# Narrow TensorE products of a hybrid decoder step widened to the whole array, and 32-column products of the recurrent stage issued together

## The chip, the cores and the metric

The kernel runs on one core of a Trainium2 chip. The metric is the device time of one execution in microseconds (us), the median over runs. TensorE is called PE in the profile, its load of the stationary operand PEld; DVE is VectorE, ACT ScalarE, POOL GpSimd, SP SyncE. In the names of products, out<-a,b has the stationary and the moving operand in either order; "128*32" are the rows and columns of the array that the stationary operand takes, and "x2" is a count of instructions. An fp32 product leaves two MATMUL records, an fp16 product one.

## The reference, cut to what matters

One layer of a decoder trunk for a prompt of 2048 tokens and a sample group of 8 sequences with 4 new tokens each (2080 token columns in all), with a past of 2048 tokens. RMSNorm, one combined input projection, two branches and an output projection:

```python
def layer_prompt(...):
    qA, kvA, gA, zA, qB, fB, iB, zB, mA, mB = project_inputs(x, norm_g, w_in)
    ctx = nsa_context(kc, vc, ks, vs, pos_k, w1_k, w2_k, pos_v, w1_v, w2_v)   # compressed blocks
    oA = nsa_attend(...) * silu(zA)       # compressed, top-8 selected and window branch, 8 heads, 2 K/V groups
    oB, S = hgrn2_branch(qB, fB, iB, zB, S0, lb, norm_g)                      # recurrence, 4 heads
    y = sigmoid(mA) * (oA @ w_ba) + sigmoid(mB) * (oB @ w_bb)
    return x + y @ w_out

# compress: out = silu(blk @ w1 + pos) @ w2, w2 is 64 x 64
# hgrn2_scan, in each chunk, with G the running sum of log decay:
A = einsum('bhtd,bhtsd,bhsd->bhts', qc, exp(D), kc)     # D = G_t - G_s for s <= t
o = einsum('bhtd,bhde->bhte', qc * exp(G), S) + einsum('bhts,bhse->bhte', A, vc)
S = exp(Gl)[..., None] * S + einsum('bhsd,bhse->bhde', kc * exp(Gl - G), vc)
```

## The kernel before

The matmuls run in fp16 pairs: an operand is split into a high and a low part (wh and wl, xh and xl), and a product is the sum of three. `mm` records a matmul, `pe.transpose` an fp32 transpose through the identity.

Stages, with their times in the profiled execution: the load of x (0 to 92 us), the compression of the sample's cache (92 to 382), bias rows (382 to 398), sample attention (398 to 640), the recurrent stage `hgrn` (640 to 1385), the start of the prompt's attention (1385 to 1600) and the rest of it with the output projection (1600 to 2467). The input projection has no stage of its own. Its products are fillers: `along(steps, ns)` goes through a stage's steps and after each issues so many nanoseconds of projection products. `feature` (L367) and `piece` (L427) make feature rows, `token` (L446) token rows.

The program is built in a context that schedules by a simulated timeline: each instruction gets a place on its engine by the code's order and by when its inputs are simulated to be ready, so code written together may be issued apart, with fillers between. Instructions under `tc.high_priority()` go ahead of others.

- `pow2_scale` (L188) turns 128 maxima, one per partition, into one power of two on all partitions: a transpose to a row (L190), DVE's maximum (L192), clamp and mask (L193, L195), a product of a one-row operand with ones (L196), DVE's scale and reciprocal (L198, L200). `pow2_of` (L216, L224) does the like for the columns of `mxs`.
- `token` multiplies 17 blocks of token rows; the last has 32.
- `hgrn` goes through 32 units (8 chunks of 256 tokens, 4 heads). `factors` makes five decay levels X0 to X4 on DVE, ACT and POOL (L717 to L721); `scores` makes, in each half of 128 tokens, one product of 64 columns and two of 32 (L740) and sixteen of 32 columns (L744) into the tile p4, from which ACT and DVE put together AT; `values` uses it. `sample_heads` does the same for the sample's 32 tokens.
- `compression` ends each of its 18 pieces with a product by w2 (L967 for keys, L977 for values), 64 rows of the array.
- `sample_attention`: `turn` transposes fetched keys (L1167), `piece` makes four products of 32 columns each, one per sequence, with 512 keys (L1190); `new` does the four new tokens (L1184).
- In the prompt phase `neg_row` (L1420) turns row maxima into rows of the queries' operand, through products with 2 or 4 stationary columns; `prep` makes the compressed branch: `cs` (L1551, L1552) scores nv = 8t + 8 compressed keys of query block t, `cpv` weighs the values, `sel` transposes the chosen blocks (L1577).

Of the kernel before, what the change touches and what calls it, by code (L numbers as in the profile page):

```python
# [10 lines left out]
F32 = mybir.dt.float32  # L11
# [42 lines left out]
def shape_constants():  # L54
# [48 lines left out]
    c["shift"] = np.tile((np.arange(256)[None, :] + np.arange(16)[:, None] == 127) * QS, (2, 1)).astype(np.float16)  # L103
# [27 lines left out]
def trunk_kernel(ctx: ExitStack, tc: tile.TileContext, A, O):  # L131
# [50 lines left out]
    ones1 = con.tile([1, 128], F32, name="ones1")  # L182
    ve.memset(ones1, 1.0)

# [3 lines left out]
    def pow2_scale(mx, pool, ps, tag):  # L188

        pe.transpose(ps[:1, 0:128], mx, ident)  # L190
        m1 = pool.tile([1, 1], F32, name=tag + "m", bufs=2)
        ve.tensor_reduce(m1, ps[:1, 0:128], axis=AX.X, op=OP.max)  # L192
        ve.tensor_scalar(m1, m1, TINY, None, op0=OP.max)  # L193
        mi = m1.bitcast(I32)
        ve.tensor_scalar(mi, mi, 0x7F800000, None, op0=OP.bitwise_and)  # L195
        mm(ps[:, 128:129], ones1, m1, True, True)  # L196
# [17 lines left out]
    def pow2_of(c0, n, ps, name):  # L214

        pe.transpose(ps[:n, 0:128], mxs[:, c0:c0 + n], ident)  # L216
# [39 lines left out]
    def make_projections(s2, st, sb):  # L256
# [3 lines left out]
        def quarter(hl, i):  # L260
            return xp.tile([128, 4352 if i == 3 else 4096], F16, name=f"x{hl}{i}")

        X4 = {hl: [quarter(hl, i).rearrange("p (k t) -> p k t", k=8) for i in range(4)] for hl in "hl"}
# [172 lines left out]
        def token(c0, n, names, ahead):  # L436
# [4 lines left out]
            for i, (t0, r) in enumerate(rows_of):  # L441
                ps = fps.tile([128, 512], F32, name="ps")[:r, :n]
                k = 0
                for kc in range(8):
                    for l, w in (("h", wh), ("h", wl), ("l", wh)):
                        mm(ps, xs(l, t0, r)[:, kc], w[:, kc], k == 0, k == 23)  # L446
                        k += 1
                    if kc == 3:
                        yield 1350
                if i == 1:  # L450
                    fetch(ahead)
# [157 lines left out]
    def hgrn():  # L609
        with ExitStack() as st:  # L610
# [32 lines left out]
            def gate_out(o_sb, zt, y, nt, r, h, t0):  # L643
# [3 lines left out]
                for j in range(nt):  # L647
                    pe.transpose(pt[:, j * 128:j * 128 + r], o_sb[:r, j], ident[:r, :r])
# [9 lines left out]

            def common(h, t0, n, L):
# [3 lines left out]
                def new(name, bufs=2):  # L663
                    return hp.tile([128, n], F32, name=name + sfx, bufs=bufs if n == NC or name == "E" else 1)
# [60 lines left out]
            def scores(u):  # L725
# [4 lines left out]
                ac.activation(u["kd"], pk[:, :NJ], AF.Copy)  # L730
                u["AT"] = []
                for j in range(NJ):
                    tj = slice(j * 128, (j + 1) * 128)
                    p4 = pa.tile([128, 4, 128], F32, name="p4")

                    near = p4[:, 1].rearrange("p (l t) -> p l t", l=4)
                    for li, L in enumerate(LEVELS[:2]):
                        X = u["Xs"][li][:, tj]
                        for s0 in range(0, 128, 2 * L):
                            mm(p4[s0:s0 + L, 0, s0 + L:s0 + 2 * L], X[:, s0:s0 + L], X[:, s0 + L:s0 + 2 * L], li == 0 or s0 == 64, True)  # L740
                    for li, (l, r) in enumerate([(x, x) for x in u["Xs"][2:]] + [(u["Bk"], u["Bq"])]):
                        for b in range(4):
                            bs = slice(j * 128 + 32 * b, j * 128 + 32 * b + 32)
                            mm(near[32 * b:32 * b + 32, li], l[:, bs], r[:, bs], li == 0 and b == 3, True)  # L744
                    AT = ATs.pop(0)
                    ATs.append(AT)
                    ac.activation(AT[:64, 2:], p4[:64, 0, 64:].rearrange("p (b t) -> p b t", t=32), AF.Copy)
                    for s0 in (0, 64):
                        ac.activation(AT[s0:s0 + 32, s0 // 32 + 1], p4[s0:s0 + 32, 0, s0 + 32:s0 + 64], AF.Copy)
# [37 lines left out]
            def sample_heads():  # L787
                for h in range(4):
                    G, qt, kt, Bq, Bk, Xo, Kd, eG = common(h, 2048, 32, 4)
                    v = hp.tile([32, 128], F32, name="vs_")  # L790
# [4 lines left out]
                    mm(pb[:32, :32], Bk, Bq, True, True)  # L795
                    AT = hp.tile([32, 32], F32, name="ATs")
# [3 lines left out]
                    mm(ov, v, AT, True, False)  # L800
                    for b in range(8):
                        mm(ov[:, 4 * b:4 * b + 4], S0[:, b], Xo[:, 4 * b:4 * b + 4], False, True)
                    oT = hp.tile([128, 32], F32, name="oT")
# [3 lines left out]
                    pe.transpose(pt[:32, :128], oT, ident)  # L807
                    o_sb = hp.tile([32, 1, 128], F32, name="o_s")
# [6 lines left out]
                    gate_out(o_sb, load_z(h, 2048, 32), y, 1, 32, h, 2048)  # L815
                    pk = po.tile([128, 512], F32, name="pk").rearrange("p (a b) -> p a b", a=4)
                    pe.transpose(pk[:32, 0], Kd, ident)
                    kd = hp.tile([32, 128], F32, name="kd_s")
# [3 lines left out]
                    for b2 in range(2):  # L822
                        vm = hp.tile([32, 4, 128], F32, name="vm", bufs=1)
# [3 lines left out]
                        mm(pu, kd, vm, True, True)  # L827
# [65 lines left out]
    def compression(seqs):  # L893
        with ExitStack() as st:
# [4 lines left out]
            for kind in "kv":  # L899
# [8 lines left out]
                w2 = cw.tile([64, 64], F32, name="w2" + kind)  # L908
                sy.dma_start(w2, A["cmp_w2_" + kind][0])
# [9 lines left out]
                ve.tensor_scalar(w2, w2, 0.5, None, op0=OP.mult)  # L919
                for s in seqs:  # L920
# [35 lines left out]
                    hb = cp.tile([64, 2, 128], F32, name="hb")  # L956
                    ac.activation(hb[:, :, :127], ph[64:128, :, 1:128], AF.Copy)
                    ve.memset(hb[:, :, 127:128], 0.0)
# [6 lines left out]
                    if kind == "k":  # L965
                        p2 = cps.tile([64, 2, 128], F32, name="p2")
                        mm(p2, w2, hb, True, True)  # L967
# [6 lines left out]
                    else:  # L974
                        p2 = cps.tile([128, 2, 64], F32, name="p2")
                        for g in range(2):
                            mm(p2[:, g], hb[:, g], w2, g == 0, True)  # L977
# [40 lines left out]
    def sample_attention():  # L1018

        with ExitStack() as st:  # L1020
# [154 lines left out]
            def logits(gb, X):  # L1175
# [5 lines left out]
                def new(kn):  # L1181
                    pq = sps.tile([128, 512], F32, name="ps", bufs=2)
                    for i, b in enumerate(bs):
                        mm(pq[32 * i:32 * i + 32, :4], queries(b), kn[:, 4 * b:4 * b + 4], True, True)  # L1184
                    return pq

                def piece(c, kts):
                    pq = sps.tile([128, 512], F32, name="ps", bufs=2)
                    for i, b in enumerate(bs):
                        mm(pq[32 * i:32 * i + 32], queries(b), kts[i], True, True)  # L1190
# [7 lines left out]
                for c in range(5):  # L1198
                    x = ready.pop(0)
                    kts = []  # L1200
                    for i in range(4):
                        kts.append(turn(x, i))
                        if i % 2:
                            yield
                            if i == 1 and last is not None:
                                piece(c - 1, last)
                    fetch()
                    last = kts
                    if c == 3:
                        pq = new(ksn)  # L1210
                        ve.scalar_tensor_tensor(S[:, 2048:], pq[:, :4], X["bm"][:, 32:33], bias[:, 128:132], op0=OP.add, op1=OP.add)
                        pq = new(kwn)
                        ve.tensor_add(Sw[:, 512:], pq[:, :4], bias[:, NB_S + 512:NB_S + NK_W])
# [189 lines left out]
    def prompt_phase(a, st, pfill, state, sw):  # L1403
# [7 lines left out]

        def neg_row(m, dst):

            n = m.shape[2]
            x = pu.tile([128, 4, 4], F16, name="xd")[:, :, :2 * n]
# [3 lines left out]
            for r in range(4):  # L1419
                mm(pt[:2 * n, r], x[:, r], a["id"], r == 0, True)  # L1420
# [49 lines left out]
        def loads(t, g, turn):  # L1470
# [6 lines left out]
            sy.dma_start(u["k"][64:96, :8 * t + 8], A["c_shift"][:, 120 - 8 * t:128])  # L1477
# [56 lines left out]
        def prep(u, t, g):  # L1534

            nv = 8 * t + 8
            nk = min(nv, 127)
# [478 lines left out]
```

## Time and profile before

| | |
|---|---|
| median of 3 runs | 2475.21 us (2474.29 to 2478.6) |
| profiled execution | 2468.52 us, span 2466.7 us, mean granted clock 0.974 |
| PE / PEld busy | 2339.0 / 1550.6 us |
| DVE / ACT / POOL busy | 1532.7 / 1182.8 / 1004.6 us |
| L744, L740 (scores) | 2048 and 384 matmul records |
| L1190 (sample logits) | 80 matmul records |
| L1420 (`neg_row`) | 256 matmul records |
| L196 (scales) | 46 matmul records |

Matmuls are pipelined: a matmul of 512 columns shows 0.38 us, but the next one starts 0.21 to 0.22 later. What one costs is read from start to start, not from its own duration.

### The profile page before, as it was taken

Reading aid. Unit: us, or ns where it says so; the run is one execution under the profiler, and the core shown is the slowest. Engines: PE = TensorE matmul, PEld = TensorE weight load, DVE = VectorE, ACT = ScalarE, POOL = GpSimd, SP = SyncE. Lnnn points to the kernel's source line nnn. Section 1 sums busy time; section 2 is a strip of 40 time slices with the busy share of each in tenths; the row PEclk is TensorE's granted clock in tenths of the full one; section 3 lists DMA queues with packets and bytes.
Section 4 is the critical chain, followed back from the end, with each engine's and each line's share of the span. In section 5 each row is a group of like instructions: output and inputs, shape, how many; then the busy total and the mean of one; then the engine's idle time right before and its main releaser. Section 6 shows DMA issues by size and latency. Waiting matters only on the chain.

```text
span 2466.7 us, 56957 instructions
## 1 busy us (share of the span) xinstructions
PE 2339.0 (95%) x22231; PEld 1550.6 (63%) x22231; DVE 1532.7 (62%) x4105; ACT 1182.8 (48%) x2605; POOL 1004.6 (41%) x1179
## 2 busy tenths in 40 slices
PE   5999999999899999999999799899999999999998
PEld 4888675555686555555665356566676666675765
DVE  7555555655623589777674356777677676767543
ACT  5544323421432256555453245445555666666663
POOL 0000102142500055554442025456665666677764
PEclk9999999999999999999999799899999999999999
DMA  6543314566852333333232433422232221211121
GB/s 204 166 129 113 126 70 144 197 229 216 251 130 74 142 132 132 107 96 122 97 118 83 114 114 117 109 78 76 60 95 73 54 76 46 69 52 47 50 58 42
DMA packets 276109, 271.78 MB, mean 110 GB/s; under 512 B 102296, under 2 KB 246176, under 8 KB 268416
## 3 DMA queue, kind: packets, MB, share of 16 engines
q1 hardware_dynamic: 267328, 230.39, 30.6%
q0 software_dynamic: 8512, 37.75, 4.5%
q8 instruction: 175, 2.87, 0.5%
q14 instruction: 94, 0.77, 0.1%
HBM read 184.54 MB, written 87.74 MB: 110 GB/s over the span
## 4 chain that ended last, share of the span: by engine, by line
PE 52%; DVE 10%; DMA 6%; ACT 3%; issue 2%; SPq 1%; POOL 1%; DVEq 0%; POOLq 0%; ACTq 0%
PE ps L367 7%; PE ps L1783 7%; PE ps L1751 7%; PE ps L427 6%; PE mx L1511 3%; PE st L1640 3%; PE st L1630 3%; PE ps L446 2%; DVE X L717 2%; PE po L1436 2%; PE po L1437 2%; PE po L1439 2%; PE mx L1513 1%; PE st L1637 1%; PE st L1636 1%
## 5 line engine op out<-in xcount | busy, mean ns | idle before, releaser
L1430 POOL TENSOR_TENSOR Pl<-P,Ph 128x512 f16<-128x512 f32 (+3 forms) x444 | 519.8, 1180 | 357.6 <-ACT Ph L1429 158.1
L1428 ACT ACTIVATE P<-st 128x512 f32<-128x512 f32 (+3 forms) x444 | 264.5, 596 | 250.1 <-PE st L1640 197.7
L367 PEld LDWEIGHTS <-wh 128*128 128x128 f16 x2240 | 216.4, 99 | 178.6 <-issue 28.1
L1429 ACT ACTIVATE Ph<-st 128x512 f16<-128x512 f32 (+3 forms) x444 | 262.7, 594 | 15.7 <-PE po L1437 13.3
L367 PE MATMUL ps<-xh,wh 128*128 128x512 f16 (+1 forms) x1120 | 232.3, 343 | 6.2 <-DVE row L389 4.6
L367 PE MATMUL ps<-xl,wh 128*128 128x512 f16 (+1 forms) x1120 | 235.9, 345 | 0.0
L367 PE MATMUL ps<-xh,wl 128*128 128x512 f16 (+1 forms) x1120 | 234.8, 343 | 0.0
L1514 DVE TENSOR_REDUCE mps<-mx 128x1 f32<-128x512 f32 (+3 forms) x320 | 186.5, 603 | 64.8 <-PE mx L1511 32.7
L446 PE MATMUL ps<-wh,xh 128*128 128x256 f16 (+3 forms) x680 | 191.8, 282 | 15.4 <-DVE row L380 6.6
L446 PE MATMUL ps<-wh,xl 128*128 128x256 f16 (+3 forms) x680 | 190.7, 281 | 4.0 <-DVE xl L333 4.0
L446 PE MATMUL ps<-wl,xh 128*128 128x256 f16 (+3 forms) x680 | 191.2, 281 | 0.0
L1436 PEld LDWEIGHTS <-Ph 128*128 128x128 f16 (+4 forms) x1776 | 139.6, 99 | 46.4 <-issue 7.7
L367 PEld LDWEIGHTS <-wl 128*128 128x128 f16 x1120 | 108.0, 99 | 86.8 <-issue 9.7
L686 POOL TENSOR_TENSOR Xo<-Xo,qt 128x256 f32<-128x256 f32 x32 | 30.2, 945 | 320.9 <-ACT Xo L685 269.8
L446 PEld LDWEIGHTS <-xh 128*128 128x128 f16 (+1 forms) x1360 | 131.7, 100 | 41.5 <-issue 16.4
L1437 PEld LDWEIGHTS <-Ph 128*128 128x128 f16 (+4 forms) x1776 | 129.4, 97 | 32.0 <-issue 0.7
L1514 DVE TENSOR_REDUCE mpw<-mx 128x1 f32<-128x512 f32 (+3 forms) x224 | 102.5, 483 | 53.0 <-PE mx L1513 52.4
L1751 PEld LDWEIGHTS <-xh 128*128 128x128 f16 x1280 | 104.4, 98 | 34.9 <-issue 9.0
L720 POOL TENSOR_TENSOR X<-X,kt 128x128 f32<-128x128 f32 x160 | 84.6, 529 | 76.4 <-ACT X L719 76.4
L1439 PEld LDWEIGHTS <-Pl 128*128 128x128 f16 (+3 forms) x1776 | 93.9, 97 | 23.7 <-POOL Pl L1430 6.7
L1436 PE MATMUL po<-vs,Ph 128*128 128x65 f16 x1088 | 105.9, 193 | 1.6 <-DVE otmp L1528 1.5
L1437 PE MATMUL po<-vs,Ph 128*128 128x64 f16 x1088 | 105.5, 193 | 0.0
(531 smaller groups left out, 5844.6 us busy)
## 6 DMA issues: line engine op xcount, KB each, us to landing
wraw<-in_w_in_dram SPq DMA_DIRECT2D x22, 1024.0 KB
xt<-in_x_prompt_dram SPq DMA_DIRECT2D x32, 512.0 KB
ma_d<-row SPq DMA_DIRECT2D x8, 1040.0 KB
out_y_prompt_dram<-xt SPq DMA_DIRECT2D x16, 512.0 KB
sg<-ma_d SPq DMA_DIRECT2D x56, 128.0 KB
sg<-mb_d SPq DMA_DIRECT2D x56, 128.0 KB
q_d<-row SPq DMA_DIRECT2D x4, 1040.0 KB
lf_d<-row SPq DMA_DIRECT2D x4, 1040.0 KB
```

The lines of the kernel that those rows point to most:

```text
L367: mm(ps, l[:, kc], xs(r, t0, n)[:, kc], k == 0, k == 23)
L427: mm(ps, l[:, kc, a * 128:(a + 1) * 128], xs(r, t0, n)[:, kc], k == 0, k == 23)
L446: mm(ps, xs(l, t0, r)[:, kc], w[:, kc], k == 0, k == 23)
L1428: ac.activation(P[:n], ps, AF.Exp, scale=1.0 / QS)
L1429: ac.activation(ph[:n], ps, AF.Exp, scale=1.0 / QS)
L1430: sub.tensor_sub(pl[:n], P[:n], ph[:n])
L1436: mm(po[:, r, :w], ph[:n, rs[r]], v[:n, :w], first and r == 0, False)
L1437: mm(po[:, r, :64], ph[:n, rs[r]], v[:n, w:w + 64], False, False)
L1439: mm(po[:, r, :w], pl[:n, rs[r]], v[:n, :w], False, last)
L1514: ve.tensor_reduce(mp_[:, r, c:c + 1], pmf[:, :n], axis=AX.X, op=OP.max)
L1751: mm(X["ps"], w[:, kc, cs], os_[o][:, kc], k == 0, k == 11)
L1783: mm(X["ps"], X["y"][y][:, kc, i0:i0 + r], W["o", kc // 4][w][:, kc % 4, cs], k == 0, k == 23)
```

## The change

- `pow2_scale`, and `pow2_of` for one column: the 128 maxima are broadcast to 128 columns and transposed, so that each partition has all of them; the one-row product goes.
- The last token block uses a stationary operand of 128 columns, zeros behind the 32 (the last quarter of x is 4448 wide).
- `sample_heads`: Bk, Kd, oT, v, AT, o, kd and vm are full tiles with zeros that POOL writes once; `gate_out` uses a product instead of a transpose there.
- `compression`: w2 and hb are 128 wide and zero outside.
- `scores`: one tile p4 for both halves. The 64-column products are split into 32-column ones, and the 40 products of a unit stand together, in groups of four column strips, under high priority, the last level (X4) first.
- Sample logits: `piece` issues its four products in the order 3, 2, 1, 0 under high priority; `new` puts both branches into one tile and is called with the piece before.
- `neg_row`: the stationary operand is a window of 128 columns in one of three tiles that are zero behind the maxima. `cs` and `cpv` use all 128 keys: the keys past nv are masked by a clipped shift operand, whose load is 32 x 128 for every block. `sel` transposes 128 columns.

```diff
     def pow2_scale(mx, pool, ps, tag):
-        pe.transpose(ps[:1, 0:128], mx, ident)
-        m1 = pool.tile([1, 1], F32, name=tag + "m", bufs=2)
-        ve.tensor_reduce(m1, ps[:1, 0:128], axis=AX.X, op=OP.max)
...
-        mm(ps[:, 128:129], ones1, m1, True, True)
+        pe.transpose(ps[:, 0:128], mx.to_broadcast([128, 128]), ident)
         un = pool.tile([128, 1], F32, name=tag + "u", bufs=3)
-        ve.tensor_scalar(un, ps[:, 128:129], 2.0 ** -14, None, op0=OP.mult)
+        ve.tensor_reduce(un, ps[:, 0:128], axis=AX.X, op=OP.max)
...
@@ token
-                        mm(ps, xs(l, t0, r)[:, kc], w[:, kc], k == 0, k == 23)
+                        x = xs(l, t0, r)[:, kc] if r == 128 else X3[l][:, kc * 544 + 512:kc * 544 + 640]
+                        mm(ps, x, w[:, kc], k == 0, k == 23)
@@ scores
+                p4 = pa.tile([128, 4, 128], F32, name="p4")
+                first = set()
+                for j in range(NJ):
+                    prod = []
+                    for li, (l, r) in reversed(list(enumerate([(x, x) for x in u["Xs"][2:]] + [(u["Bk"], u["Bq"])]))):
+                        for b in range(4):
+                            bs = slice(j * 128 + 32 * b, j * 128 + 32 * b + 32)
+                            prod.append((b, p4[32 * b:32 * b + 32, 2 * j + 1, 32 * li:32 * li + 32], l[:, bs], r[:, bs]))
+                    prod = prod[4:8] + prod[:4] + prod[8:]
+                    for li, L in enumerate(LEVELS[:2]):
+                        X = u["Xs"][li][:, j * 128:(j + 1) * 128]
+                        for s0 in range(0, 128, 2 * L):
+                            for c0 in range(s0, s0 + L, 32):
+                                prod.append((c0 // 32, p4[c0:c0 + 32, 2 * j, s0 + L:s0 + 2 * L], X[:, c0:c0 + 32], X[:, s0 + L:s0 + 2 * L]))
+                    with tc.high_priority():
+                        for b, o, l, r in prod:
+                            mm(o, l, r, b not in first, True)
+                            first.add(b)
...
-                            mm(p4[s0:s0 + L, 0, s0 + L:s0 + 2 * L], X[:, s0:s0 + L], X[:, s0 + L:s0 + 2 * L], li == 0 or s0 == 64, True)
...
-                            mm(near[32 * b:32 * b + 32, li], l[:, bs], r[:, bs], li == 0 and b == 3, True)
@@ sample_heads
-                    mm(pb[:32, :32], Bk, Bq, True, True)
+                    mm(pb[:, :32], WIDE["Bk"], Bq, True, True)
@@ compression
-                        mm(p2, w2, hb, True, True)
+                        p2 = cps.tile([128, 2, 128], F32, name="p2")
+                        mm(p2, w2, hb_, True, True)
+                        p2 = p2[:64]
@@ logits
-                    for i, b in enumerate(bs):
-                        mm(pq[32 * i:32 * i + 32], queries(b), kts[i], True, True)
+                    with tc.high_priority():
+                        for i in (3, 2, 1, 0):
+                            mm(pq[32 * i:32 * i + 32], queries(bs[i]), kts[i], True, True)
...
                             if i == 1 and last is not None:
                                 piece(c - 1, last)
+                                if c == 3:
+                                    pn = new()
@@ neg_row
-                mm(pt[:2 * n, r], x[:, r], a["id"], r == 0, True)
+                mm(pt[:, r], xd[:, 2 * n * r:2 * n * r + 128], a["id"], r == 0, True)
@@ query block's operands
-            sy.dma_start(u["k"][64:96, :8 * t + 8], A["c_shift"][:, 120 - 8 * t:128])
+            sy.dma_start(u["k"][64:96], A["c_shift"][:, 120 - 8 * t:248 - 8 * t])
@@ prep
-                mm(ps[:nv], KB["c", g][:, :nv], flat(u["b"]), True, False)
-                mm(ps[:nv], u["k"][:, :nv], flat(u["c"]), False, True)
-                X["p"] = probs(ps[:nk], nk, pu, (1, 1), gp)
+                mm(ps, KB["c", g], flat(u["b"]), True, False)
+                mm(ps, u["k"], flat(u["c"]), False, True)
+                X["p"] = probs(ps, 128, pu, (1, 1), gp)
...
-                pv(po, *X["p"], V["c"][:, g], nk, 97, True, True)
+                pv(po, *X["p"], V["c"][:, g], 128, 97, True, True)
```

How instructions move on TensorE, at three places. First the scores, in a unit of the second chunk's time: before, single products of the tile p_9011 stand between token products (L446, fillers), here one of them.

```order
L446 LDWEIGHTS xl_127
L446 MATMUL ps<-wh,xl_127 128x256
L744 MATMUL p_9011<-X_8927 32x32
L446 LDWEIGHTS xh_123
L446 MATMUL ps<-wh,xh_123 128x256
```

After the change, L767 holds all score products; here those of a unit's two halves, between a product of AT and one of the state (L794, L796).

```order
L794 MATMUL ov<-v,AT_8648 128x128
L767 MATMUL p_9462<-X_9445 32x32 x4
L767 MATMUL p_9462<-Bq,Bk 32x32 x4
L767 MATMUL p_9462<-X_9439 32x32 x4
L767 MATMUL p_9462<-X_9433 32x32 x4
L767 MATMUL p_9462<-X_9421 32x64 x2
L767 MATMUL p_9462<-X_9427 32x32 x2
L767 MATMUL p_9462<-X_9445 32x32 x4
L767 MATMUL p_9462<-Bq,Bk 32x32 x4
L767 MATMUL p_9462<-X_9439 32x32 x4
L767 MATMUL p_9462<-X_9433 32x32 x4
```

Products that stood in single places between fillers now stand in one row.

The sample logits on TensorE, where keys are transposed (L1167 into pkt) beside projection products (L367): before, the products with 512 keys come two at a time.

```order
L1184 MATMUL ps<-ksn,Q 32x4 x4
L1167 MATMUL pkt<-ident,kvr 128x128 x8
L1190 MATMUL ps<-kts,Q 32x512 x2
L367 LDWEIGHTS wh
L367 MATMUL ps<-xl_127,wh 128x512
```

After, four at a time (L1232), and the new tokens' products (L1224) of both branches stand together; L1206 is the transpose, L375 the filler.

```order
L375 MATMUL ps<-xl_125,wh 128x512
L1206 MATMUL pkt<-ident,kvr 128x128 x4
L1232 MATMUL ps<-kts,Q 32x512 x4
L1206 MATMUL pkt<-ident,kvr 128x128 x4
L1224 MATMUL ps<-ksn,Q 32x4 x4
L1224 MATMUL ps<-kwn,Q 32x4 x4
```

The piece's two visits have become one.

The prompt phase's start on TensorE, where `neg_row` and `cs` follow the maxima of the compressed branch (L1543): before, two stationary columns and 32 key rows.

```order
L1420 LDWEIGHTS xd
L1420 MATMUL mx<-h_id,xd 2x128
L1420 LDWEIGHTS xd
L1420 MATMUL mx<-h_id,xd 2x128
L1551 LDWEIGHTS kbc_6582
L1551 MATMUL st<-qb,kbc_6582 32x512
```

After, at the same place, 128 of each (L1470, L1600).

```order
L1470 LDWEIGHTS xd_16458
L1470 MATMUL mx<-h_id,xd_16458 128x128
L1470 LDWEIGHTS xd_16458
L1470 MATMUL mx<-h_id,xd_16458 128x128
L1600 LDWEIGHTS kbc_6527
L1600 MATMUL st<-qb,kbc_6527 128x512
```

The order of the rows stays; their shapes change.

More of the change, by code (lines that the diff above doesn't have):

```diff
@@ L214, in pow2_of @@
     def pow2_of(c0, n, ps, name):
+        if n == 1:
+            pe.transpose(ps[:, 0:128], mxs[:, c0:c0 + 1].to_broadcast([128, 128]), ident)
+            out = con.tile([128, 1], F32, name=name)
+            ve.tensor_reduce(out, ps[:, 0:128], axis=AX.X, op=OP.max)
+            ve.tensor_scalar(out, out, TINY, None, op0=OP.max)
+            oi = out.bitcast(I32)
+            ve.tensor_scalar(oi, oi, 0x7F800000, None, op0=OP.bitwise_and)
+            return out
         pe.transpose(ps[:n, 0:128], mxs[:, c0:c0 + n], ident)
@@ L260, in quarter @@
         def quarter(hl, i):
-            return xp.tile([128, 4352 if i == 3 else 4096], F16, name=f"x{hl}{i}")
-        X4 = {hl: [quarter(hl, i).rearrange("p (k t) -> p k t", k=8) for i in range(4)] for hl in "hl"}
+            return xp.tile([128, 4448 if i == 3 else 4096], F16, name=f"x{hl}{i}")
+        X4 = {hl: [quarter(hl, i) for i in range(4)] for hl in "hl"}
+        X3 = {hl: X4[hl][3] for hl in "hl"}
+        X4 = {hl: [x[:, :4352 if i == 3 else 4096].rearrange("p (k t) -> p k t", k=8) for i, x in enumerate(X4[hl])] for hl in "hl"}
+        for hl in "hl":
+            ve.memset(X3[hl][:, 4352:], 0.0)
         def xs(hl, t0, n):
@@ L441, in token @@
             for i, (t0, r) in enumerate(rows_of):
-                ps = fps.tile([128, 512], F32, name="ps")[:r, :n]
+                ps = fps.tile([128, 512], F32, name="ps")[:, :n]
                 k = 0
@@ L647, in gate_out @@
                 for j in range(nt):
-                    pe.transpose(pt[:, j * 128:j * 128 + r], o_sb[:r, j], ident[:r, :r])
+                    if r == 128:
+                        pe.transpose(pt[:, j * 128:j * 128 + r], o_sb[:, j], ident)
+                    else:
+                        mm(pt[:, j * 128:j * 128 + r], o_sb[:, j], ident[:, :r], True, True)
                 n = (nt - 1) * 128 + r
@@ L741, in scores @@
[L741 to L744, printed above, removed]
+                    near = p4[:, 2 * j + 1].rearrange("p (l t) -> p l t", l=4)
                     AT = ATs.pop(0)
                     ATs.append(AT)
-                    ac.activation(AT[:64, 2:], p4[:64, 0, 64:].rearrange("p (b t) -> p b t", t=32), AF.Copy)
+                    ac.activation(AT[:64, 2:], p4[:64, 2 * j, 64:].rearrange("p (b t) -> p b t", t=32), AF.Copy)
@@ L806, in sample_heads @@
                     pt = po.tile([128, 512], F32, name="pk")
-                    pe.transpose(pt[:32, :128], oT, ident)
-                    o_sb = hp.tile([32, 1, 128], F32, name="o_s")
+                    pe.transpose(pt[:, :128], WIDE["oT"], ident)
+                    o_sb = o_[:32]
                     ss = hp.tile([32, 1], F32, name="ss_s")
```

92 lines of the change are left out of this document (51 added, 41 removed).

## The prediction

> **What bounds the kernel now.** I read the page's busy times and its chain first, then a table by stage, then the rows of the products that the diff touches.
>
> ```profile
> PE 2339.0 (95%) x22231; PEld 1550.6 (63%) x22231; DVE 1532.7 (62%) x4105; ACT 1182.8 (48%) x2605; POOL 1004.6 (41%) x1179
> PE 52%; DVE 10%; DMA 6%; ACT 3%; issue 2%; SPq 1%; POOL 1%; DVEq 0%; POOLq 0%; ACTq 0%
> ```
>
> TensorE is busy for 95% of the span and has half of the chain that ended last; no other engine comes near. So TensorE's time is what a change can take away. How much of it reaches the end differs by stage (columns: stretch, its length, busy us and instructions of PE, PEld, DVE, ACT and POOL, the granted clock, the DMA share, GB/s):
>
> ```profile
> 0.00:92.00 92.00, 66.42 (x504) 56.39 (x505) 64.35 (x161) 47.73 (x87) 1.92 (x8) 0.93 0.55 171
> 92.00:382.00 290.00, 288.87 (x2209) 227.57 (x2207) 150.53 (x411) 113.29 (x185) 23.46 (x19) 1.00 0.38 117
> 398.00:640.00 242.00, 233.80 (x1663) 128.61 (x1661) 138.00 (x277) 64.65 (x77) 71.04 (x68) 0.99 0.63 214
> 640.00:1385.00 745.00, 705.37 (x6392) 449.44 (x6390) 474.31 (x1282) 350.65 (x1089) 273.69 (x464) 0.97 0.38 119
> 1385.00:1600.00 215.00, 185.09 (x1799) 112.73 (x1798) 125.97 (x413) 100.03 (x172) 80.72 (x82) 0.88 0.43 120
> 1600.00:2467.00 867.00, 843.40 (x9597) 568.28 (x9595) 572.19 (x1548) 505.09 (x994) 553.78 (x538) 1.00 0.22 62
> ```
>
> The compression (92 to 382) is never without TensorE work; the sample attention (398 to 640) misses 8 us, the recurrent stage (640 to 1385) 40, the start of the prompt phase (1385 to 1600) 30, the rest of it 24.
>
> Busy is not streaming, though. The price that the change goes for is seen only in start times, since a matmul's end is modelled. Three wide rows around one lone 32-column product of the recurrent stage:
>
> ```profile
> 709.07 0.27 PE L446 MATMUL ps<-wl,xh 128*128 128x256 f16 x1
> 709.18 0.27 PE L446 MATMUL ps<-wh,xl 128*128 128x256 f16 x1
> 709.38 0.25 PE L744 MATMUL p<-X 128*32 128x32 f32 x2
> 709.56 0.28 PE L446 MATMUL ps<-wh,xh 128*128 128x256 f16 x1
> ```
>
> Two wide L446 products start 0.11 apart. Before the L744 product the start is 0.20 later, so entering a 32-column shape costs about 0.09; leaving it costs 0.09 again, and the whole visit is 0.38 - 0.11 = 0.27 us, of which some 0.08 is the product. Over all changes of shape in the trace I find 93 to 97 ns each; I use 0.094 us. The same surplus stands around the other narrow products:
>
> ```profile
> 1862.62 0.38 PE L1783 MATMUL ps<-xh,yh 128*128 128x512 f16 x1
> 1862.83 0.38 PE L1783 MATMUL ps<-xl,yh 128*128 128x512 f16 x1
> 1863.14 0.39 PE L1420 MATMUL mx<-h_id,xd 128*4 128x128 f16 x4
> 1863.46 0.39 PE L1783 MATMUL ps<-xh,yl 128*128 128x512 f16 x1
> 1863.68 0.38 PE L1783 MATMUL ps<-xh,yh 128*128 128x512 f16 x1
> ```
>
> L1783 takes 0.21 to 0.22 between starts; before the four L1420 products of `neg_row` it is 0.31, and these four take 0.32, that is 4 x 0.055 and one change more.
>
> **Part by part.** I counted changes of shape along TensorE's order in both kernels (the column-narrow fp32 transposes left out, whose row stands with the third rival): 708 before, 158 after.
>
> *The recurrent stage's scores.* 102 visits become 33, and 270 changes 66, because the 64-column products go too: 204 x 0.094 = 19.2 us. Side by side they also run faster:
>
> ```profile
> 660.74 0.27 PE L446 MATMUL ps<-wh,xl 128*128 128x256 f16 x1
> 660.94 0.33 PE L744 MATMUL p<-X 128*32 128x32 f32 x16
> ...
> 661.36 0.25 PE L744 MATMUL p<-Bq,Bk 128*32 128x32 f32 x6
> 661.54 0.28 PE L446 MATMUL ps<-wh,xh 128*128 128x256 f16 x1
> ```
>
> Between the first and the last of these rows lie 26 products (two records each) in 0.60 us, 0.023 each where the lone one took 0.08. 197 products stand before the change in visits of eight or fewer; 197 x 0.057 = 11 if each was alone, nothing if those were already abreast. I take 8, nearer the upper end since 24 of the 102 visits hold just one. Together 27, between 19 and 30.
>
> *The sample logits.* A visit has one price whatever it holds:
>
> ```profile
> 442.18 1.06 PE L1190 MATMUL ps<-kts,Q 128*32 128x512 f32 x8
> 443.18 0.75 PE L367 MATMUL ps<-xh,wl 128*128 128x272 f16 x5
> ...
> 444.73 1.05 PE L1190 MATMUL ps<-kts,Q 128*32 128x512 f32 x4
> 445.72 0.39 PE L367 MATMUL ps<-xh,wh 128*128 128x512 f16 x1
> ```
>
> Four products (eight records) take 1.00 to the next start, two take 0.99; with the late entry it is 1.07. The order has 22 visits before and ten after, each of four: 12 x 1.07 = 12.8. The new tokens' logits go from four visits to two at 0.27: 0.5. Sum 13.3; its lower end is 12 x 0.19 = 2.3, if the products themselves were hidden, which the rows exclude as TensorE does nothing else meanwhile.
>
> *neg_row, cs and cpv* become wide: 117.5 and 78.5 changes go, 11.0 and 7.4 us. The products keep their streams, since the moving operand is the same. What widens is the load of the stationary operand:
>
> ```profile
> L1420 PEld LDWEIGHTS <-xd x256: 79/83/128, 1395.4 to 2355.5; 128*2 128x2 f16 x64, 128*4 128x4 f16 x64
> L1543 PEld LDWEIGHTS <-qc x128: 95/98/151, 1392.1 to 2231.0; 96*128 96x128 f16 x128
> ```
>
> Two or four columns load in 83 ns, 128 in 98 (the medians). 256 x 15 ns = 3.8 us if loads set the pace; they run beside the products, PEld is busy for 63%, so I take 0. The Trainium skill ("TensorE: Matmul & The Clock Gate", LDWEIGHTS) puts a load at its columns over 1.2 ns, so by that rule 256 loads would grow by 103 ns, 26 us in all, more than these edits bring; the two rows disagree with it, and the sum goes by them. The masked keys add rows to the work behind: `probs` and the POOL subtraction go to 128 rows, which changes no row's length in elements, and the key load becomes 32 rows of 128 columns in one DMA: 0, hidden by prefetch.
>
> *The scales.* Each of 25 calls loses its one-row product:
>
> ```profile
> 333.89 0.38 PE L367 MATMUL ps<-xh,wl 128*128 128x512 f16 x1
> 334.20 0.38 PE L196 MATMUL tp<-wxm,ones 1*128 1x1 f32 x2
> 334.51 0.39 PE L367 MATMUL ps<-xh,wl 128*128 128x512 f16 x1
> ```
>
> 0.62 from start to start where 0.22 is usual: 25 x 0.40 = 10.0. DVE keeps its five instructions; the scale comes a TensorE round trip earlier. The transpose now has 128 columns, and the row under the third rival prices it as free.
>
> *The rest.* 36 changes at the compression's second product (L967, L977), 26 at the sample's recurrent heads, 10 at the last token rows and 6 at the sample's values: 78 x 0.094 = 7.3. The new memsets run once, on POOL and DVE, which have room: 0. Holding a piece's four sample products until the last block's keys are there costs nothing while L367 fills the gap.
>
> Sum of TensorE time: 27 + 13.3 + 18.4 + 10.0 + 7.3 = 76 us, between 59 (19 for the scores, two changes alone for each scale, 3.8 of longer loads) and 79 (30 for the scores).
>
> **What reaches the end.** By stage the 76 split into 1 (load), 6.3 (compression), 15.9 (sample attention), 34 (recurrent stage), 9 (start of the prompt phase) and 10 (rest). The compression passes all on. The sample attention is also fed by gathers, so 12.5. In the recurrent stage an idle 40 us shows that units wait for DVE, POOL and DMA in places; time saved there turns into a longer wait. Its chain is TensorE for most pieces but DVE's decay factors and score masks for the next largest share, so I pass 70%: 24. The start of the prompt phase is 14% idle and waits on transfers: half, 4.5. The rest: 9.5. Sum 1 + 6.3 + 12.5 + 24 + 4.5 + 9.5 = 58. The profiled execution (span 2466.7, run 2468.5) would come to 2410; it lies 6.7 below the median of the runs, and against that median of 2475.2 the forecast is 2417 us.
>
> **The rivals.**
>
> *Only the full stretches pass it on.* If the recurrent stage and the start of the prompt phase are set by other engines, 24 and 4.5 vanish: -29, 2446. For it: DVE is busy 474 of 745 us there, and the 40 idle us. Against: DVE has 270 us free, and the chain's largest pieces in that stretch are projection products. 0.19.
>
> *All of it is passed on*, since filler products fill any hole: -76 to -79, 2397. For it: the compression at 289 of 290 us. 0.16.
>
> *The change doesn't do what it says*: the surplus comes from small fp32 products as such, not from the shape. Then zeros and copies buy nothing, and only removed work counts: 12.8 and 10.0, three quarters of it, -17: 2458. Against it is a small fp32 transpose from one column between wide products,
>
> ```profile
> 1291.18 0.27 PE L190 MATMUL tp<-ident,wmx 128*1 128x128 f32 x1
> 1291.29 0.28 PE L427 MATMUL ps<-xh,wh 128*128 128x272 f16 x1
> ```
>
> which passes in 0.11 with no surplus, while the fp16 products of L1420 show it. A page speaks against it too: "Changing tiling mode (not just tile) drains the TensorE" (the Trainium skill, "TensorEngine Tiling (Array Packing)", Key Properties), with which the 0.09 at each border agrees. 0.04.
>
> *Slower: the score group stands in front of TensorE.* All 40 products of a unit are now one block at high priority, so TensorE waits at its first product for POOL's last multiplication, where before the fillers between the products bridged it.
>
> ```profile
> 652.55 0.45 POOL L720 TENSOR_TENSOR X<-X,kt 128x128 f32<-128x128 f32 x1
> ...
> 656.22 0.91 POOL L720 TENSOR_TENSOR X<-X,kt 128x128 f32<-128x128 f32 x1
> ```
>
> ```profile
> PE p L744 <- POOL X L721: 1.4, 4, 0.6
> ```
>
> The first two rows are POOL's: it takes about 3.7 us from a unit's second level to its last. The last row is from the waits of TensorE (total, times, longest). If each of 32 units stood for all of it: +118 - 58 = +60, 2535; at 1.8 us a unit it eats the whole gain, and there it decides. Against it: before, the trace has 1.4 us of such waits in all, and in the new order only three of the 32 groups hold a wait behind their first product. 0.09, of which 0.03 ends within 0.2% (what a measurement of this kernel can tell from no change, 5 us).
>
> **How the numbers follow.** Forecast 0.52, the rivals 0.19, 0.16, 0.04, 0.09. The range reaches from full conversion (2397, less 3 for longer groups abreast) to the first rival (2446) with 4 us for its share of the load: 2394 to 2450, 0.87 of the cases. Faster: 0.52 + 0.19 + 0.16 + 0.04 = 0.91; same 0.03; slower 0.06.
>
> **What would show it.** Between starts: wide products 0.11 or 0.22 apart around the products of `neg_row`, `cs` and `cpv`, with no 0.09 on either side; some 33 score visits near 1.1 us; ten sample visits of eight records; no one-row product of the scales. By stage: the compression shorter by 6, the sample attention by 12, the recurrent stage by 24, the prompt phase by 14. The prediction is wrong if score visits open with waits of microseconds on POOL, if the idle 40 us of the recurrent stage grow to 70, or if loads of 128 columns push the products behind them apart.

## The result, and the profile after

| | before | after | ratio (95% interval) |
|---|---|---|---|
| median of 4 runs each | 2476.90 us | 2436.41 us | 0.9836 (0.9814 to 0.9859) |
| profiled execution, span | 2466.7 us | 2430.0 us | |

The change makes the kernel 40 us faster; the forecast was 58, the range 2394 to 2450. On a second chip the ratio was 0.9828 (0.9814 to 0.9842). A comparison of runs below goes by the ratio to the kernel before on the same chip, since that kernel itself took 2462 to 2476 us on the chips used. One run of the narrow probe below took 6784 us, its nine others 2459 to 2474; it is left out of that kernel's ratio.

The page after, in the same two lines as shown of before:

```profile
PE 2261.2 (93%) x22313; PEld 1541.8 (63%) x22313; DVE 1549.8 (64%) x4088; ACT 1180.3 (49%) x2606; POOL 1014.7 (42%) x1192
PE 70%; DVE 12%; DMA 7%; ACT 4%; issue 3%; SPq 2%; POOL 1%; another core or an unknown queue 0%; ACTq 0%; DVEq 0%; POOLq 0%
```

TensorE's busy time fell by 78 us, the span by 37. The four products of `neg_row` among products of 512 columns, after the change:

```profile
1823.83 0.38 PE L1834 MATMUL ps<-xl,yh 128*128 128x512 f16 x1
1824.04 0.39 PE L1470 MATMUL mx<-h_id,xd 128*128 128x128 f16 x4
1824.27 0.38 PE L1834 MATMUL ps<-xh,yl 128*128 128x512 f16 x1
1824.48 0.38 PE L1834 MATMUL ps<-xh,yh 128*128 128x512 f16 x1
```

The start before them is 0.21, as between any two L1834, and they take 0.23 where they took 0.32: both surpluses of 0.09 are gone. A unit's 40 score products, first row, last row and the next filler:

```profile
655.26 0.27 PE L767 MATMUL p<-X 128*32 128x32 f32 x8 [0.70 <-POOL X L739]
...
655.81 0.49 PE L767 MATMUL p<-X 128*32 128x32 f32 x23
656.23 0.28 PE L456 MATMUL ps<-wh,xl 128*128 128x256 f16 x1
```

They take 0.97 us from first start to the next product, 0.024 each. Before the first of them TensorE waited 0.70 us for POOL.

To see where the 78 us went, I split each gap between two matmul starts into work and idle: what a gap has beyond the stream counts as idle when it is more than 0.3 us, and otherwise as work (the changes of shape are in it). I put the borders of the stages at the same events in both kernels (the first product of the compression, of the bias rows, of the compressed branch's sums; the last of sample attention and of the recurrent stage; the first of the output projection):

| us | before: length, idle | after: length, idle | length |
|---|---|---|---|
| load | 97.3, 19.5 | 97.0, 21.9 | -0.3 |
| compression | 295.6, 1.4 | 287.4, 1.1 | -8.2 |
| bias rows, start of sample attention | 42.6, 0.9 | 51.3, 9.4 | +8.7 |
| sample attention | 182.0, 9.0 | 166.1, 6.0 | -15.9 |
| recurrent stage | 760.2, 45.0 | 746.7, 63.8 | -13.5 |
| border and start of the prompt phase | 192.2, 31.7 | 186.9, 43.2 | -5.3 |
| rest of the prompt phase | 896.8, 22.9 | 894.8, 28.3 | -2.0 |
| sum | 2466.7, 130.4 | 2430.0, 173.8 | -36.7 |

Work fell by 80.1 us; idle time rose by 43.4. So the question is not whether the work left TensorE, but why over half of it came back as waiting. Waits of TensorE (total, times, longest), first before, at the border to the prompt phase, then after, at the border and for the recurrent stage:

```profile
PE mx L1543 <- DMA qc<-tc_d: 9.9, 4, 5.5
```

```profile
PE mx L1592 <- DMA qc<-tc_d: 17.3, 3, 13.8
...
PE pu L863 <- DVE own L778: 7.4, 3, 3.6
PE ov L660 <- DVE o_sb L656: 7.4, 3, 5.9
...
PE p L767 <- DVE own L780: 5.1, 2, 4.2
PE ov L794 <- DVE zt L665: 4.9, 4, 2.6
...
PE p L767 <- POOL X L739: 3.8, 6, 1.2
```

At the border only 0.6 us of projection products stand behind the recurrent stage's last product, where 8.6 stood before, and TensorE then waits 13.8 us for the first query block's load, where it waited 5.5 before. The next four are in the recurrent stage, all for DVE: together 24.8 us, where the same four were 13.9 before. The score products' own wait for POOL grew from 1.4 to 3.8 us only.

### The profile page after: what moved, and what is told of

Same layout as the page of the kernel before. It is cut to its first block, busy times and chain, and to the rows that moved or that the text cites. A ratio compares the mean times of both kernels' runs of the same rounds, so it can differ in the third digit from the quotient of the medians.

```text
span 2430.0 us, 57057 instructions
## 1 busy us (share of the span) xinstructions
PE 2261.2 (93%) x22313; PEld 1541.8 (63%) x22313; DVE 1549.8 (64%) x4088; ACT 1180.3 (49%) x2606; POOL 1014.7 (42%) x1192
## 4 chain that ended last, share of the span: by engine, by line
PE 70%; DVE 12%; DMA 7%; ACT 4%; issue 3%; SPq 2%; POOL 1%; another core or an unknown queue 0%; ACTq 0%; DVEq 0%; POOLq 0%
PE ps L375 16%; PE ps L1834 7%; PE ps L456 7%; PE ps L1802 6%; PE ps L435 6%; PE st L1691 3%; PE st L1681 3%; PE mx L1561 3%; DVE X L735 3%; PE ph L994 2%; PE po L1486 2%; PE po L1487 2%; PE po L1489 2%; DMA wraw<-in_w_in_dram 1%; PE pt L977 1%
## 5 line engine op out<-in xcount | busy, mean ns | idle before, releaser
L1480 POOL TENSOR_TENSOR Pl<-P,Ph 128x512 f16<-128x512 f32 x444 | 520.4, 1182 | 313.2 <-ACT Ph L1479 175.2
L1478 ACT ACTIVATE P<-st 128x512 f32<-128x512 f32 x444 | 264.9, 597 | 246.8 <-PE st L1691 190.4
L375 PEld LDWEIGHTS <-wh 128*128 128x128 f16 x2240 | 221.6, 100 | 178.2 <-issue 21.9
L1479 ACT ACTIVATE Ph<-st 128x512 f16<-128x512 f32 x444 | 263.0, 595 | 11.6 <-PE po L1487 9.4
L375 PE MATMUL ps<-xh,wh 128*128 128x512 f16 (+1 forms) x1120 | 232.6, 346 | 8.2 <-DVE row L397 5.4
L375 PE MATMUL ps<-xl,wh 128*128 128x512 f16 (+1 forms) x1120 | 235.1, 346 | 1.2 <-issue 1.2
L375 PE MATMUL ps<-xh,wl 128*128 128x512 f16 (+1 forms) x1120 | 233.3, 344 | 0.0
L456 PE MATMUL ps<-wh,xh 128*128 128x256 f16 (+1 forms) x680 | 190.7, 280 | 11.9 <-ACT to L464 7.4
L456 PE MATMUL ps<-wh,xl 128*128 128x256 f16 (+1 forms) x680 | 189.7, 279 | 4.0 <-DVE xl L341 4.0
L456 PE MATMUL ps<-wl,xh 128*128 128x256 f16 (+1 forms) x680 | 190.4, 280 | 0.0
L1486 PEld LDWEIGHTS <-Ph 128*128 128x128 f16 x1776 | 140.4, 99 | 41.4 <-ACT Ph L1479 5.8
L375 PEld LDWEIGHTS <-wl 128*128 128x128 f16 x1120 | 111.0, 100 | 81.8 <-issue 3.3
L456 PEld LDWEIGHTS <-xh 128*128 128x128 f16 x1360 | 132.7, 100 | 34.9 <-issue 10.5
L1487 PEld LDWEIGHTS <-Ph 128*128 128x128 f16 x1776 | 129.3, 97 | 33.0 <-issue 0.7
L1802 PEld LDWEIGHTS <-xh 128*128 128x128 f16 x1280 | 105.1, 98 | 34.4 <-issue 10.2
L1489 PEld LDWEIGHTS <-Pl 128*128 128x128 f16 x1776 | 94.7, 98 | 25.9 <-POOL Pl L1480 9.0
L1681 PE MATMUL st<-qb,kbs 128*128 128x512 f16 x272 | 103.0, 379 | 2.6 <-ACT Ph L1479 2.4
```

Source lines behind the costliest of these rows:

```text
L375: mm(ps, l[:, kc], xs(r, t0, n)[:, kc], k == 0, k == 23)
L456: mm(ps, x, w[:, kc], k == 0, k == 23)
L1478: ac.activation(P[:n], ps, AF.Exp, scale=1.0 / QS)
L1479: ac.activation(ph[:n], ps, AF.Exp, scale=1.0 / QS)
L1480: sub.tensor_sub(pl[:n], P[:n], ph[:n])
L1486: mm(po[:, r, :w], ph[:n, rs[r]], v[:n, :w], first and r == 0, False)
```

## The experiments

### What a change of shape costs by itself

Into the compression, where TensorE is never idle, go 198 products that nobody reads, narrow in one kernel, wide in the other.

```diff
+            probe = cw.tile([128, 128], F16, name="probe")
...
                                 mm(ph, l[:, 2 * j2 + j], r[:, j], k == 0, k == 23)
                                 k += 1
+                                if k % 2 == 0 and k < 24:
+                                    mm(pj[:32, :64], probe[:, :32], probe[:, 64:128], True, True)
```

The wide kernel has 128 in place of 32.

> The changed kernel with 198 products more in the compression, whose TensorE is never idle: fp16, a stationary operand of 32 columns, 64 moving columns, written to a place that nothing reads. They stand in 125 visits between wide products. Shape theory: 125 x 0.188 = 23.5 us for the changes of shape and 198 x 0.03 to 0.055 = 6 to 11 for the products: 30 to 34 us longer than the changed kernel. Rival (a small product costs that as such, whatever its shape): the same as the wide probe.

> The same 198 products at the same places with a stationary operand of 128 columns. Shape theory: only the products' own 6 to 11 us, 23 us less than the narrow probe. Rival: as long as the narrow probe, some 30 us over the changed kernel.

Ratios to before: narrow 1.0011 (0.9996 to 1.0027), wide 0.9915 (0.9890 to 0.9940). One place in the narrow kernel, then in the wide one:

```profile
104.90 0.28 PE L997 MATMUL ph<-Rh,cwl 128*128 128x256 f32 x1
105.11 0.20 PE L1000 MATMUL p<-probe 128*32 128x64 f16 x1
105.24 0.39 PE L997 MATMUL ph<-Rl,cwh 128*128 128x256 f32 x1
105.47 0.28 PE L997 MATMUL ph<-Rh,cwh 128*128 128x256 f32 x1
```

```profile
104.75 0.28 PE L997 MATMUL ph<-Rh,cwl 128*128 128x256 f32 x1
104.88 0.20 PE L1000 MATMUL p<-probe 128*128 128x64 f16 x1
104.92 0.36 PE L997 MATMUL ph<-Rl,cwh 128*128 128x256 f32 x1
105.12 0.28 PE L997 MATMUL ph<-Rh,cwh 128*128 128x256 f32 x1
```

From L997 to the next L997 it is 0.34 us over the narrow product and 0.17 over the wide one. The compression takes 325.8 and 300.4 us: 25.4 over 125 visits is 0.203 us a visit, 0.10 a change. The medians differ by 26.5 us. The shape is the cause of these 25 us, and not that the product is small, since the wide one is as small; that rival is excluded. What the Trainium skill says ("TensorEngine Tiling (Array Packing)", Key Properties: a change of tiling mode drains the engine) fits this, and the price of it here is 0.09 to 0.10 us a border. The wide probes cost 13 us by the compression's length (300.4 against 287.4 in the changed kernel's profile), more than the 6 to 11 expected.

### neg_row narrow again

```diff
-                mm(pt[:, r], xd[:, 2 * n * r:2 * n * r + 128], a["id"], r == 0, True)
+                mm(pt[:2 * n, r], xd[:, 2 * n * r:2 * n * r + 2 * n], a["id"], r == 0, True)
```

> The changed kernel with neg_row's stationary operand 2 or 4 columns wide again, all else kept: some 61 visits pay two changes of shape, 11.5 us of TensorE. Theory A (the prompt phase has waits that absorb it, as nothing was gained between 1600 us and the end): 0 to 5 us longer than the changed kernel. Theory B (the gain there was eaten by another part of the change, the wider cs and cpv above all): 9 to 12 us longer, 2446.

0.9868 (0.9853 to 0.9883), 0.0032 above the changed kernel, some 8 us; the interval overlaps that of the changed kernel's first measurement a little, and not that of its second (0.9814 to 0.9842). TensorE's work rose by 12.7 us, its idle time fell by 4.7; the rest of the prompt phase was 6.3 us longer. That lies between the two theories and nearer B: here most of the gain does arrive. What ate the rest of the prompt phase's gain is not shown; `cs` and `cpv` were not made narrow again.

### The scores alone, and all but the scores

```diff
@@ scores, in the kernel before; in the changed kernel the reverse
-                            mm(near[32 * b:32 * b + 32, li], l[:, bs], r[:, bs], li == 0 and b == 3, True)
+                    with tc.high_priority():
+                        for b, o, l, r in prod:
+                            mm(o, l, r, b not in first, True)
```

> The kernel before with the new scores alone; its order has 33 score visits instead of 101. Theory A (the work leaves TensorE, and the recurrent stage gives about half of it back as waiting on DVE and POOL): TensorE streams 27 to 35 us less, its idle time grows by 12 to 20, and the run is 10 to 18 us shorter, near 2462. Theory B (it all arrives): 27 to 35 us shorter, near 2446. Theory C (the high-priority block makes TensorE stand for POOL and eats the gain): no shorter, 2472 or more.

> The changed kernel with the old scores; 100 score visits instead of 33. Theory A: 10 to 18 us longer than the changed kernel, 2446 to 2454. Theory B: 27 to 35 longer, near 2467. Theory C: the same as the changed kernel or shorter, 2436 or less.

Alone, the new scores gain 0.44% (0.9956, 0.9943 to 0.9970), 12 us of the 31 that TensorE's work falls. But the changed kernel without them is at 0.9802 (0.9789 to 0.9816): no slower than with them, by the middle 8 us faster, with intervals that just touch. Theory A holds for the first and theory C for the second; no theory holds for both. The parts do not add up, and on top of the others the grouped scores, with their priority, bring nothing.

### The scores without their priority

```diff
-                    with tc.high_priority():
-                        for b, o, l, r in prod:
-                            mm(o, l, r, b not in first, True)
-                            first.add(b)
+                    for b, o, l, r in prod:
+                        mm(o, l, r, b not in first, True)
+                        first.add(b)
```

> The changed kernel without the high priority around the score products; all of them stay 32 columns wide, but the order has 111 visits instead of 33. Theory A: as with the old scores, 10 to 18 us longer than the changed kernel. Theory B: 25 to 35 longer. Theory C (priority costs): 5 us shorter or more, 2431 or less.

0.9740 (0.9727 to 0.9753): 62 us faster than before and some 22 faster than the changed kernel, although the products stand in 111 visits again. Theory C holds. Against the old scores in the changed kernel (0.9802) the new products without priority win some 15 us. TensorE's work is 17 us more than in the changed kernel, its idle time 34 less. The stretch from the first to the last product of the score matrices with the values, in the kernel before, the changed one and this one:

```profile
861.00:1354.00 493.00, 462.93 (x4550) 285.01 (x4549) 359.92 (x1047) 271.26 (x925) 235.95 (x406) 0.96 0.35 111
```

```profile
834.00:1322.00 488.00, 443.90 (x4648) 283.04 (x4647) 374.49 (x1061) 272.25 (x928) 239.88 (x406) 0.95 0.35 112
```

```profile
842.00:1290.00 448.00, 409.97 (x4447) 261.02 (x4446) 357.14 (x1045) 264.87 (x918) 237.22 (x406) 0.97 0.37 115
```

In the changed kernel the score products of this stretch take 27 us instead of 46, but projection products fill part of what was saved (333 us of them after 327), idle time most of the rest (49 us by the gaps, after 35), and the stretch is hardly shorter. Without priority it is 40 us shorter, with 292 us of projection products; the rest of them is left for the start of the prompt phase, which has waits to fill: its idle time is 21 us instead of 43.

### Is it the amount of projection products?

```diff
-        fill(350.0)
+        fill(12350.0)
```

> The changed kernel with 12 us more of projection products taken before the prompt phase's start, where TensorE waited 14 us for the first query block's load. If that wait is a hole which the old amount of fillers no longer covers (theory A): 6 to 10 us shorter than the changed kernel, near 2428, with that wait under 5 us. If the fillers are missed later (rival): within 3 us of the changed kernel, with the idle time turning up between 1400 and 1560 us.

0.9811 (0.9794 to 0.9828), by the middle 6 us better than the changed kernel, though the intervals overlap; that is between the two expectations. The border and the start are 25 us shorter, the rest of the prompt phase 21 longer: most is missed later. The longest wait for the query block's load is still 13.8 us, so the added products did not go into it. Then the amount asked for behind each step of the recurrent stage, with and without the scores' priority:

```diff
-        along(hgrn(), 1250.0)
+        along(hgrn(), 500.0)
```

With priority this was run with 500 and 1500, without it with 1500.

> The changed kernel with its high priority kept, but with 500 instead of 1250 ns of projection products asked for behind each step of the recurrent stage. In its order 276 us of them stand between the first and the last product of the score matrix with the values, as in the version without priority (276), and not 313 as in the changed kernel. Theory D (what the priority costs is only that it lets projection products run out too early, which the start of the prompt phase then lacks): 15 to 25 us shorter than the changed kernel, near 0.974 of before, with idle TensorE near 140 us. Theory E (the block itself costs, by making every unit wait for its last level): the same as the changed kernel within 5 us, 0.984 of before.

> The version without priority around the scores, with 1500 ns asked for behind each step: 304 us of projection products in that stretch instead of 276. Theory D: most of the gain over the changed kernel goes, 0.981 to 0.984 of before. Theory E: it stays, 0.974 of before.

> The changed kernel, high priority kept, with 1500 ns of projection products asked for behind each step of the recurrent stage: the fourth cell beside priority with 1250 (0.983 of before) and none with 1250 (0.974) and 1500 (0.967). Theory E (the block of 40 products costs whatever the fillers): 0.980 to 0.985 of before, the recurrent stage's chunks still near 67 us apart, TensorE idle over 155 us. Theory F (1500 is the better dose for either order, and the priority costs only at the old dose): 0.967 to 0.972, idle under 130 us.

| ratio to before (95%) | 500 | 1250 | 1500 |
|---|---|---|---|
| with priority | 0.9813 (0.9799 to 0.9826) | 0.9836; again 0.9828 | 0.9810 (0.9792 to 0.9829) |
| without | | 0.9740 (0.9727 to 0.9753) | 0.9666 (0.9650 to 0.9682) |

Theory D is wrong: with 500 the stretch has as few projection products (292 us) as without priority, and nothing is won beyond the spread; the idle time turns up inside it (57 us by the gaps, 49 in the changed kernel, 43 without priority). Theory E holds with priority at each amount. That 1500 without priority would be faster still was in neither theory. It is the best version of all, 81 us under the kernel before. The row of the same stretch in it, and then the row with priority and 500:

```profile
829.00:1277.00 448.00, 427.52 (x4576) 273.76 (x4574) 355.13 (x1044) 268.18 (x924) 237.56 (x406) 0.98 0.38 121
```

```profile
820.00:1278.00 458.00, 407.57 (x4445) 262.86 (x4444) 358.59 (x1027) 263.28 (x918) 237.18 (x406) 0.94 0.35 111
```

TensorE is busy 428 of 448 us in the one, 408 of 458 in the other, with the same DVE and POOL work. So without priority the stretch takes 448 us with 292 us of projection products and with 316; with priority it takes 458 with 292.

### Without any priority

```diff
-                    with tc.high_priority():
-                        for i in (3, 2, 1, 0):
-                            mm(pq[32 * i:32 * i + 32], queries(bs[i]), kts[i], True, True)
+                    for i in (3, 2, 1, 0):
+                        mm(pq[32 * i:32 * i + 32], queries(bs[i]), kts[i], True, True)
```

> The version without priority around the scores, and without it around the sample attention's four-column-strip products too; the stretch of the recurrent stage has 275 us of projection products as without it there. If priority does nothing for the sample logits: within 3 us of the version without priority around the scores, 0.974 of before. If the ten whole visits come apart again into some twenty: 8 to 12 us longer, 0.978 of before.

0.9848 (0.9834 to 0.9861), 27 us longer than with the sample logits' priority kept. The size was not expected, nor the place: the sample logits still stand in ten visits, sample attention is 2 us shorter in its profile, and the recurrent stage 26 us longer (15 of them ahead of its first product with the values). The kernel is then no faster than the changed one, although no product has priority: what the scores' priority costs was measured with the sample logits' priority in place, and does not hold for every order. So a stage's order also hangs on what the scheduler did ahead of it.

### What the orders have in common

From the start of a unit's decay sums (DVE, tile G) to the end of its products with the values, the median over units 8 to 31, from the traces:

| | us per unit | last score to values |
|---|---|---|
| before | 62.2 | 42.4 |
| scores with priority: alone; changed; 500; 1500 | 63.7; 61.5; 61.0; 62.7 | 49.5; 47.6; 46.0; 48.3 |
| without: old scores; 1250; 1500; none at all | 56.7; 57.0; 56.2; 57.6 | 34.5; 37.9; 19.0; 38.0 |

With priority a unit's scores are ready 46 to 50 us before they are used, and the unit takes 61 to 64 us, in each of the four orders. Without it, in the kernel with the change's other parts, both are shorter: 19 to 38 and 56 to 58. The kernel before has no priority and 62.2; what the other parts win of that, the priority takes back. This is shown by four orders against four; why it does so is not. Nor does the unit's time by itself set the kernel's: with priority and 500 a unit takes 61.0 us and the stretch is only 458, and without any priority it takes 57.6 and the kernel is no faster than the changed one. A possible reason for the long units is that DVE then assembles the score matrices early, in a queue of its own in which other units' work stands behind them, and the four AT tiles hold two units only. A larger ring of AT tiles was not tried on the chip.

### The changed kernel once more

> The changed kernel once more, for a second profile and as the measure for the other three on this chip. If the stall of about 8 us between 404 and 416 us, in which TensorE, VectorE and ScalarE all crawl while the first keys are gathered, belongs to the program, it stands again; if it comes and goes, it is part of the run-to-run spread. Time: 0.984 of the kernel before.

0.9828, and no stall: between 404 and 416 us TensorE was idle for 7.4 us in the first profile (first row), and hardly in the second.

```profile
404.00:416.00 12.00, 4.63 (x28) 1.95 (x25) 1.32 (x5) 2.39 (x4) 6.80 (x8) 0.89 0.65 204
```

```profile
404.00:416.00 12.00, 11.84 (x82) 6.61 (x83) 8.22 (x21) 8.83 (x12) 9.15 (x9) 1.00 0.92 324
```

So the stall belongs to some executions and not to the program; its rows and where it stood follow in the last section.

## Why the prediction was right in what leaves TensorE and wrong in the share that arrives

- **The price of a border.** 0.094 us a change from the start times; 0.10 by the probes. Right, and that the shape is its cause is shown. The scales, the sample's heads, the last token rows, and `cs` and `cpv` were not undone one by one.
- **TensorE's time.** 76 us were summed, 80.1 less work was measured (compression 7.9 against 6.3, sample attention 12.9 against 15.9, recurrent stage 32.3 against 34, border and start 16.8 against 9, rest 7.4 against 10; at the border 9 us are projection products, 64 us of them after 73). The wider loads cost nothing that shows:

```profile
L1470 PEld LDWEIGHTS <-xd x256: 95/98/184, 1366.5 to 2319.8; 128*128 128x128 f16 x128
```

  The median is 98 ns, as bounded from L1543, and the products' median from start to start is 0.055 us before and 0.056 after. The Trainium skill's rule ("TensorE: Matmul & The Clock Gate", LDWEIGHTS), under which 256 loads would grow by 26 us, does not hold for the narrow ones: 2 or 4 columns took 83 ns, not 2 or 3.
- **What reaches the end: the step that failed.** 58 of 76 us were to arrive; 36.7 of 80 did. The mis-sized terms are the recurrent stage, 24 predicted and 13.5 measured, and the rest of the prompt phase, 9.5 and 2.0; another 8.7 us went in a stall (next point). Why the rest of the prompt phase gave so little stays open: its work fell by 7.4 us and its idle time rose by 5.4. The term of the recurrent stage was argued from TensorE's share of the chain and DVE's free time: 70% of what is saved. That reasoned as if the order around the products stayed. It did not: with the scores' priority a unit takes as long as before, and what the scores saved is filled by projection products and idle time, and is idle time where the projection products are few (500). From the end of sample attention to the end of the kernel the profiles give 1849.2 us before, 1828.3 after and 1810.1 without the scores' priority: 20.9 and 39.1 won, where 38 were predicted. That the version without priority meets the 38 is in part luck, since without any priority this part takes 1832.1. The prediction's own sign of this, 40 idle us of the recurrent stage growing to 70, did not appear in full: by busy time over the same borders they grew from 40 to 57.
- **Sample attention** was to give 12.5. The stretch behind the bias rows gave 15.9, but 8.7 us were lost ahead of it, in a stall which the second profile of the same kernel does not have.
- **The rivals.** The one in which only the full stretches pass their gain on (2446) came nearer than the forecast (2417), by its number alone: it gave nothing to the recurrent stage and the start of the prompt phase, which won 13.5 and 5.3, and all of its 9.5 to the rest, which won 2.0. The slower one, TensorE standing in front of the score group, was priced as waits for POOL; these grew to 3.8 us, far from the 58 that would decide. But its cause, the high priority, is what cost most: some 22 us by the version without it, which goes with units that take longer and not with a wait that can be seen at the group. Full conversion would have been 2397; the version without priority took 2414.1 us, where the kernel before took 2476.4.
- **Same or slower** was given 0.09, and the interval excludes both.

The profile of before held the products' price, and could not show this: its waits belong to an order in which fillers stood around each score product. Read for another order, the 1.4 us for POOL said nothing on how long a unit would take in it.

## What to carry to other kernels

Read small products from start to start: if a narrow one pushes its neighbours apart by 0.1 us on each side, zero columns that made it as wide as its neighbours removed that here at no cost that showed, and the gain arrived whole where TensorE is always busy (the compression). Where a scheduler fills in other work, the engine's share of the chain does not tell how much of a saving arrives: look as well at how long one unit takes from its first step to its last, and at the idle time inside the stage. Try a group both with and without priority, and with more and fewer fillers: here the same products, split into 111 visits again, made the kernel 22 us faster, and with a larger dose of fillers 38 (2385.04 against 2422.93 us on one chip).

## What the hardware showed that was not expected

Around 404 to 416 us, while the first selected keys are gathered, TensorE, VectorE and ScalarE all crawl in some executions, with gaps of 1.0 to 1.2 us between single matmuls for which no releaser is shown:

```profile
409.06 0.38 PE L375 MATMUL ps<-xl,wh 128*128 128x512 f16 x1 [1.16 <-issue]
410.47 0.18 PE L1158 MATMUL ps<-gates,k_rtok 32*128 32x24 f32 x1 [1.03 <-issue]
411.87 0.18 PE L1158 MATMUL ps<-gates,k_rtok 32*128 32x24 f32 x1 [1.22 <-issue]
416.16 1.97 PE L1206 MATMUL pkt<-ident,kvr 128*128 128x128 f32 x8 [4.12 <-DVE kts L1209]
```

It cost some 8 us in the profiles of the changed kernel and of the four experiments on the scores and `neg_row`, all taken where the kernel before needs 2476 us; it is in none of the eight taken where that needs 2462 to 2466, and not in the profile of before. Whether it is the chip or the moment, and what the engines wait for, stays open.
